# Four single PSUM banks in place of two bank pairs in the gate and up products of a hybrid encoder

## The chip, the cores and the metric

The kernel runs on one core of one Trainium2 chip. The metric is the device time of one execution in microseconds, as the median of several runs. TensorE (PE) does the matrix products; its sequence of weight loads is shown apart as PEld. VectorE (DVE) and ScalarE (ACT) read PSUM, GpSimd (POOL) works in SBUF alone, and SyncE (SP) issues most of the DMAs.

## The reference, cut to what matters

Two encoder layers, 1024 tokens of width 1024 in fp32. Each layer has a mixer stage, a gated MLP and a gated input embedding. The change touches the first two products of the MLP:

```python
D_FF = 2816
for i in range(DEPTH):                      # DEPTH = 2
    ...
    gate = dwconv_centred(h @ ffn_w_gate[i], ffn_conv_w[i], ffn_conv_b[i])
    f = (jax.nn.silu(gate) * (h @ ffn_w_up[i])) @ ffn_w_down[i]
    h = layer_norm(ALPHA * h + f, ln2_g[i], ln2_b[i])
    ...
```

## The kernel before, in words

**Work and tiles.** The kernel is written with pools of tiles; a scheduler then sets the order of the instructions on each engine, from the program's order and from what each one must wait for. Each fp32 operand is split into a high and a low part (`split`, L82: ACT copies the high part, another engine subtracts), and one product of two such operands is three matmuls (`p3`).

**The gate and up products** are in `gate_up` (L1355), once for each layer. The 2816 hidden features are taken in 22 blocks of 128. One block's up weights and gate weights together are a matrix of two block rows; the tokens' transposed activations are cut in two by two blocks. Block by block, they are multiplied by a scheme with seven products instead of eight: `product` (L1380) is 4 times `p3`, that is 12 matmuls of 128x128 by 128x512 into one PSUM bank of 128x512 fp32. Seven operands on the token side are kept for the whole stage: the tiles named `x` in the trace are B11, B21, 22 and t1, and those named `xq` are t2, t3 and t4. The weight side is made anew for each feature (`feature`, L1398): two DMAs bring the raw up and gate weights (`wraw`), sums and differences are taken, and `part` (L1375) splits them into the tiles `w`. For the first three features the two products with B11 and B21 are made ahead (`starts`, L1466), while the other token operands are still being built from transposes (L1473 to L1486).

**PSUM.** There are eight banks. The pool `ps1` gives single banks (tile `ps`, four of them, `one()`), the pool `ps2` pairs of banks (tile `pp`, two of them, `two()`). In `feature` two pairs are taken: `pa` (L1413) takes the product with t2 in its first half and that with t1 in its second, `pb` (L1426) that with t4 and that with 22. The products with t3, B11 and B21 take single banks:

```python
pa = self.two()
u = small()
self.tt(u, product(w2, B["t2"], pa[:, lo]), v1, add)
u4 = small()
self.tt(u4, product(w1, B["t1"], pa[:, hi]), u, add)
```

Each product is read from PSUM by DVE, which adds it to an earlier result (tiles `u`, `v`, `g`); the one with B11 is copied by ACT (`v1`).

**What follows a feature.** `gated` (L1432) takes the convolution and the SiLU of the gate and multiplies by up; `paired` (L1444) stores sums and differences of two features to DRAM (`fp`, from the tiles `u` and `k`) for the down projection. The down projection (`down_paired`, from L1546 on; its matmuls are L1613) starts with operands called `part`, made of `fr` (read back from `fp`) and of the down weights (`wr`, `wraw`); its first product takes both bank pairs.

**Queues.** SP issues its DMAs in the order in which the scheduler put them, weight loads and stores among each other, and a DMA whose data is not ready holds up those behind it.

Of the kernel before, what the change touches and what calls it, by code (L numbers as in the profile page):

```python
# [2 lines left out]

# [7 lines left out]
F32 = mybir.dt.float32  # L11
# [4 lines left out]
PSUM = bass.MemoryType.PSUM  # L16
# [58 lines left out]
class Trunk:  # L75
# [32 lines left out]

    def two(self):
        return self.ps2.tile([128, 1024], F32, name="pp", tag="pp")  # L110

    def load_w(self, src, shape, pool=None, tag="whl", eng=None, bufs=None):
        nc = self.nc
        raw = self.wp.tile(shape, F32, name="wraw", tag="wraw", bufs=2)
        nc.sync.dma_start(raw, src)
        pool = pool or self.wp
        kw = {"bufs": 4} if pool is self.wp else {"bufs": bufs} if bufs else {}
        hi = pool.tile(shape, F32R, name="wh", tag=tag, **kw)
        lo = pool.tile(shape, F32R, name="wl", tag=tag, **kw)
        self.split(hi, lo, raw, eng or nc.gpsimd)  # L120
        return hi, lo
# [107 lines left out]
    def build(self):  # L229
        tc, ctx = self.tc, self.ctx  # L230
        self.ps1 = self.pool(ctx, "ps1", 4, space=PSUM)
        self.ps2 = self.pool(ctx, "ps2", 2, space=PSUM)
        self.dram = self.pool(ctx, "dram", 1, space=DRAM)
        self.sm = self.pool(ctx, "sm", 2)
        self.small_constants()
        self.wp = self.pool(ctx, "wp", 2)
        self.xp = self.pool(ctx, "xp", 8)
        self.khat = [[self.dram.tile([128, 3 if q == 0 else 2, 512], F32, name=f"khat{l}_{q}")
                      for q in range(8)] for l in range(L)]
        x = None  # L240
        for l in range(L):
            with ExitStack() as st:
                mu = self.pool(st, f"mu{l}")
                late = None
                if l == 0:
                    x, late = self.embed()
                else:
                    x, late = nxt
                rows = self.mixers(l, x, mu, late, st)
            hst = ExitStack()  # L250
            mid = self.out_proj(l, hst, *rows)
            nxt = self.rest(l, hst, *mid)
# [1102 lines left out]
    def gate_up(self, l, H, hp, x, fd):  # L1355
# [4 lines left out]
        add, sub = ALU.add, ALU.subtract  # L1360
        fd, fp = fd
        kept = []
        with ExitStack() as st:
# [4 lines left out]
            B = {"11": x[0], "21": x[1]}  # L1368

            def load(n, f):  # L1370
                w = self.wp.tile([128, 1024], F32, name="wraw", tag="wraw", bufs=2)
                nc.sync.dma_start(w.rearrange("p (k m) -> p k m", k=8), t[n][l, f])
                return w[:, 0:512], w[:, 512:1024]
# [3 lines left out]
                self.split(w[:, 0], w[:, 1], src, eng or nc.gpsimd)  # L1377
                return w

            def product(w, b, ps=None):  # L1380
                ps = self.one() if ps is None else ps
                wh, wl = [w[:, i].rearrange("p (k m) -> p k m", k=4) for i in range(2)]
                self.mm(ps, [z for k in range(4) for z in self.p3(wh[:, k], wl[:, k], b[0][:, k], b[1][:, k])])
                return ps

            def first(w1, w2, eng=None):

                v1, c11 = small(), fu.tile([128, 512], F32, name="u", tag="u", bufs=6)
                self.act(v1, product(part(w1, self.wp, "whl", eng), B["11"]))

                def second():
                    self.tt(c11, product(a12, B["21"]), v1, add)
                    return c11

                a12 = part(w2, self.wp, "whl", eng)
                return v1, second

            def feature(f, last, start=None):  # L1398
                a11, a12 = load("ffn_w_up", f)
                a21, a22 = load("ffn_w_gate", f)  # L1400
                v1, c11 = start or first(a11, a12)
                s1 = fu.tile([128, 512], F32, name="s", tag="s", bufs=1)
                self.tt(s1, a21, a22, add)
                w1 = part(s1, hp, "H")
                self.tt(a21, a11, a21, sub)
                self.tt(a11, s1, a11, sub, nc.gpsimd)
                w2 = part(a11, hp, "H", nc.vector)
                w3 = part(a21, hp, "H", nc.vector)
                w22 = part(a22, hp, "H")
                self.tt(a12, a12, a11, sub, nc.gpsimd)  # L1410
                w4 = part(a12, hp, "H")
                lo, hi = slice(0, 512), slice(512, 1024)
                pa = self.two()  # L1413
                u = small()
                self.tt(u, product(w2, B["t2"], pa[:, lo]), v1, add)
                u4 = small()
                self.tt(u4, product(w1, B["t1"], pa[:, hi]), u, add)
                if last:
                    gated(*last)
                g = big()  # L1420
                p7 = product(w3, B["t3"])
                self.tt(g[:, 512:1024], p7, u4, add)
                self.tt(u, p7, u, add)
                if start is None:
                    c11 = c11()
                pb = self.two()  # L1426
                self.tt(g[:, 0:512], product(w22, B["t4"], pb[:, lo]), u, add)
                c12 = fu.tile([128, 512], F32, name="u", tag="u", bufs=6)
                self.tt(c12, product(w4, B["22"], pb[:, hi]), u4, add)
                return f, g, c11, c12  # L1430

            def gated(f, g, *cc):  # L1432
                tg = big()
                self.conv3(tg, g, pp[:, C_FFC + 4 * f:C_FFC + 4 * f + 4])
                self.act(tg, tg, AF.Silu)
                for hf, c in enumerate(cc):
                    cs = slice(hf * 512, (hf + 1) * 512)
                    self.tt(c, c, tg[:, cs], ALU.mult, nc.gpsimd if hf else nc.vector)
                    if f >= PAIRED:
                        nc.sync.dma_start(fd[f][:, cs], c)  # L1440
                if f < PAIRED:
                    paired(f, *cc)
# [21 lines left out]
                    put(3, s4)  # L1464

            starts = []  # L1466
            for f in range(3):
                v1, c11 = first(*load("ffn_w_up", f), nc.vector)
                starts.append((v1, c11()))
# [3 lines left out]
            for j in range(4):  # L1473
                h0, h1 = H[j], H[j + 4]
                a, b = slice(0, 512), slice(512, 1024)
# [9 lines left out]
                self.blocks([(d[:, b], p2[:, a], B["t3"]), (d[:, a], p2[:, b], B["t2"])], j)  # L1485
                self.blocks([(h0[:, b], self.one(), B["t4"])], j)  # L1486
            last = None
            for f in range(NF):
                last = feature(f, last, starts[f] if f < 3 else None)
            gated(*last)  # L1490

    def down(self, l, fd, hmid, H, end, ed):
        nc, t, pp = self.nc, self.t, self.pp[l]
# [341 lines left out]
```

## Time and profile before

| | us |
|---|---|
| median of 3 runs | 3204.69 |
| these runs | 3196.22 to 3207.54 |
| the profiled execution, its own time | 3194.46 |
| its span | 3192.7 |
| PE busy in the span | 2946.4 (92%) |
| DVE busy | 2440.4 (76%) |
| POOL busy | 1771.2 (55%) |
| ACT busy | 1291.6 (40%) |
| gate and up, layer 0: from the first product with a token operand made of a transpose to the end of the last | 813.8 to 1245.0 |
| gate and up, layer 1: the same | 2390.5 to 2822.0 |

An engine that waits is idle in these numbers, so the share of busy time says which engine is nearest to being the bound, but not which waits matter. The ends of matmuls are modelled in the trace, so the pace of PE is best read from the starts of matmuls that follow each other. The granted clock of TensorE is either full (2.4 GHz, shown as 1.00) or half (1.2 GHz), and a stretch shows the mean.

### The profile page before, as it was taken

To read this page: it belongs to the slowest core of one execution; us is meant where nothing else is said; L and a number is where in the kernel's file an instruction comes from. 1 tells how busy PE (TensorE), PEld (TensorE's weight loads), DVE (VectorE), ACT (ScalarE), POOL (GpSimd) and SP (SyncE) were. 2 spreads that over 40 slices of the span, in tenths; PEclk is the share of its full clock that TensorE was granted. 3 is DMA by queue.
4 is the path that set the end of the run, shared out by engine and by line. 5 is a ranking of instruction groups with operands and counts; after the bars stand their busy time and mean duration, and the time that the engine had idled before them with its cause. 6 is when DMAs were issued, how large, how long until landed. Compare 5 with 4: busy or idle time off the path is not lost.

```text
span 3192.7 us, 40546 instructions
## 1 busy us (share of the span) xinstructions
PE 2946.4 (92%) x14316; PEld 2420.9 (76%) x14316; DVE 2440.4 (76%) x3711; ACT 1291.6 (40%) x2278; POOL 1771.2 (55%) x1371
## 2 busy tenths in 40 slices
PE   6999988999899999999989998889989999999996
PEld 4887866877678777787867877768767787777785
DVE  7678786878766777889777786868786677768986
ACT  4332365743333334443342333667333333344341
POOL 5455533527555666887435463335185556679845
PEclk9999998999999999999999998999999999999998
DMA  5466523022233326523335664130322333274332
GB/s 181 152 202 213 180 85 137 16 84 86 76 99 106 102 96 225 189 93 124 114 107 159 219 215 158 53 122 17 107 73 83 99 111 99 101 257 146 106 132 89
DMA packets 153427, 400.44 MB, mean 125 GB/s; under 512 B 16578, under 2 KB 43462, under 8 KB 152968
## 3 DMA queue, kind: packets, MB, share of 16 engines
q1 hardware_dynamic: 138968, 347.18, 32.5%
q0 software_dynamic: 14256, 50.67, 5.2%
q8 instruction: 114, 1.87, 0.2%
q14 instruction: 89, 0.73, 0.1%
HBM read 294.50 MB, written 103.28 MB: 125 GB/s over the span
## 4 chain that ended last, share of the span: by engine, by line
PE 48%; DVE 22%; POOL 9%; DMA 8%; issue 8%; ACT 5%; SPq 0%; DVEq 0%; POOLq 0%; ACTq 0%
PE ps L99 17%; PE pp L99 15%; PE ps L1613 7%; DMA wraw<-in_ffn_w_gate_dram 4%; POOL H L87 2%; DVE g L90 2%; DVE u L87 2%; PE ps L942 2%; DVE w L87 2%; POOL w L87 2%; DVE H L90 2%; PE ps L1054 1%; DVE v L87 1%; ACT w L84 1%; POOL wraw L87 1%
## 5 line engine op out<-in xcount | busy, mean ns | idle before, releaser
L99 PE MATMUL pp<-x,wh 128*128 128x512 f32 x1344 | 430.0, 398 | 1.8 <-ACT wh L84 1.8
L1613 PE MATMUL ps<-part 128*128 128x512 f32 x1440 | 341.4, 393 | 14.7 <-DVE H L87 6.1
L87 POOL TENSOR_TENSOR w<-wraw,w 128x512 fp32r<-128x512 f32 x164 | 232.7, 1431 | 206.0 <-ACT w L84 205.8
L1613 PEld LDWEIGHTS ps<-part 128*128 128x128 f32 x1440 | 270.8, 189 | 78.4 <-DVE H L87 9.8
L99 PEld LDWEIGHTS pp<-x,wh 128*128 128x128 f32 x1344 | 256.1, 193 | 54.2 <-ACT wh L84 2.0
L99 PE MATMUL ps<-x,w 128*128 128x512 f32 x1056 | 261.6, 395 | 10.8 <-ACT v L84 10.8
L99 PE MATMUL pp<-x,w 128*128 128x512 f32 x1056 | 258.3, 394 | 14.1 <-DVE v L87 9.7
L99 PE MATMUL pp<-x,wl 128*128 128x512 f32 x672 | 266.8, 397 | 3.8 <-POOL wl L87 3.8
L99 PE MATMUL pp<-xq,w 128*128 128x512 f32 x1056 | 264.4, 392 | 5.8 <-DVE x L87 4.5
L84 ACT ACTIVATE w<-wraw 128x512 fp32r<-128x512 f32 x264 | 152.8, 622 | 267.6 <-DMA wraw<-in_ffn_w_up_dram 169.9
L87 POOL TENSOR_TENSOR wl<-wraw,wh 128x1024 fp32r<-128x1024 f32 (+2 forms) x61 | 153.6, 2520 | 173.6 <-ACT wh L84 119.8
L99 PEld LDWEIGHTS pp<-x,w 128*128 128x128 f32 x1056 | 196.9, 188 | 63.7 <-DVE v L87 13.8
L87 POOL TENSOR_TENSOR part<-fr,part 128x512 fp32r<-128x512 f32 x140 | 220.5, 1602 | 43.7 <-ACT part L84 43.4
L99 PEld LDWEIGHTS ps<-x,w 128*128 128x128 f32 x1056 | 199.0, 190 | 59.9 <-ACT v L84 18.0
L99 PEld LDWEIGHTS pp<-xq,w 128*128 128x128 f32 x1056 | 198.0, 188 | 51.2 <-ACT w L84 5.1
L99 PE MATMUL ps<-wo,yn 128*128 128x512 f32 x768 | 188.0, 401 | 5.5 <-DVE H L90 3.1
L87 DVE TENSOR_TENSOR part<-wr,part 128x512 fp32r<-128x512 f32 x124 | 155.5, 1278 | 39.0 <-ACT part L84 38.7
L1039 POOL TENSOR_TENSOR P<-P,smr 128x1024 f32<-128x1024 f32 x64 | 121.2, 1895 | 110.1 <-DVE smr L1038 101.2
L99 PEld LDWEIGHTS ps<-wo,yn 128*128 128x128 f32 x768 | 145.4, 193 | 39.6 <-DVE H L90 5.4
L99 PE MATMUL ps<-wh,x 128*128 128x512 f32 x512 | 158.7, 390 | 0.0
L99 PEld LDWEIGHTS pp<-x,wl 128*128 128x128 f32 x672 | 129.1, 192 | 30.6 <-POOL wl L87 4.7
L90 DVE SCALAR_TENSOR_TENSOR g<-g,pp 128x1023 f32<-128x1023 f32 x88 | 128.4, 1460 | 27.0 <-ACT g L84 25.6
(385 smaller groups left out, 7264.5 us busy)
## 6 DMA issues: line engine op xcount, KB each, us to landing
fr<-fp SPq DMA_DIRECT2D x70, 512.0 KB, 3.7
c_fwd<-in_c_fwd_dram POOLq DMA_DIRECT2D x64, 512.0 KB, 5.4
wraw<-in_ffn_w_up_dram SPq DMA_DIRECT2D x50, 512.0 KB, 3.5
fp<-u SPq DMA_DIRECT2D x100, 256.0 KB, 2.4
wraw<-in_ffn_w_gate_dram SPq DMA_DIRECT2D x44, 512.0 KB, 3.8
wraw<-in_w_in_dram SPq DMA_DIRECT2D x42, 512.0 KB, 3.7
wr<-in_ffn_w_down_dram SPq DMA_DIRECT2D x36, 512.0 KB, 4.8
c_inv<-in_c_inv_dram POOLq DMA_DIRECT2D x32, 512.0 KB, 4.8
```

Source lines behind the costliest of these rows:

```text
L84: self.nc.scalar.activation(out, in_, func, **kw)
L87: (eng or self.nc.vector).tensor_tensor(out, a, b, op=op)
L90: return self.nc.vector.scalar_tensor_tensor(out, a, s, b, op0=op0, op1=op1)
L99: ins = self.nc.tensor.matmul(out, a, b, start=i == 0, stop=i == n - 1)
L942: ins = self.nc.tensor.matmul(out[0:64] if j else out, v[:, 0, :] if j else v.rearrange("p i d -> p (i d)"), terms[i][1 + j], start=k == 0 ...
L1039: nc.gpsimd.tensor_tensor(P, P, sm.to_broadcast([128, T]), op=ALU.mult)
L1054: nc.tensor.transpose(pt[:, j * 128:(j + 1) * 128], P[:, c0:c0 + 128], self.ident)
L1613: nc.tensor.matmul(ps, u, v, start=k == 0 and (p != 1 or ch == 0), stop=k == 5 and (p != 1 or ch == last))
```

## The change

From `feature(0)` on, the pool of two bank pairs is closed and a pool of four single banks takes its place (tile `pt`). `product` takes its bank by turns from this pool and from the four `ps` banks; `turn` is constant 0 before that point, so that the products made ahead still take `ps`. After the last `gated` the pairs come back. What is computed is the same; the scheduler orders the changed program anew.

```diff
+    def swap2(self, name, bufs):
+
+        self.st2.close()
+        self.ps2 = self.st2.enter_context(self.tc.tile_pool(name=name, bufs=bufs, space=PSUM, reuse_waits="tile"))
...
         self.ps1 = self.pool(ctx, "ps1", 4, space=PSUM)
-        self.ps2 = self.pool(ctx, "ps2", 2, space=PSUM)
+        self.st2 = ctx.enter_context(ExitStack())
+        self.ps2 = self.pool(self.st2, "ps2", 2, space=PSUM)
...
-            def product(w, b, ps=None):
-                ps = self.one() if ps is None else ps
+            def product(w, b):
+                if next(turn):
+                    ps = self.ps2.tile([128, 512], F32, name="pt", tag="pt")
+                else:
+                    ps = self.one()
...
-                lo, hi = slice(0, 512), slice(512, 1024)
-                pa = self.two()
                 u = small()
-                self.tt(u, product(w2, B["t2"], pa[:, lo]), v1, add)
+                self.tt(u, product(w2, B["t2"]), v1, add)
                 u4 = small()
-                self.tt(u4, product(w1, B["t1"], pa[:, hi]), u, add)
+                self.tt(u4, product(w1, B["t1"]), u, add)
...
-                pb = self.two()
-                self.tt(g[:, 0:512], product(w22, B["t4"], pb[:, lo]), u, add)
+                self.tt(g[:, 0:512], product(w22, B["t4"]), u, add)
                 c12 = fu.tile([128, 512], F32, name="u", tag="u", bufs=6)
-                self.tt(c12, product(w4, B["22"], pb[:, hi]), u4, add)
+                self.tt(c12, product(w4, B["22"]), u4, add)
...
+            turn = itertools.repeat(0)
...
             last = None
+            turn = itertools.cycle((1, 0))
+            self.swap2(f"ps3_{l}", 4)
             for f in range(NF):
                 last = feature(f, last, starts[f] if f < 3 else None)
             gated(*last)
+            self.swap2(f"ps2_{l}", 2)
```

Three places show how the order moves. In all of them the number behind `w_` names one product's weights, and `x12` means twelve matmuls in a row.

**A feature in the steady part, on PE** (layer 0, feature 5). Before, weights 8416 belong to B21, 8421 to t1, 8426 to t2, 8429 to t3 and 8432 to t4 of this feature; 8543 and 8573 are B11 and t3 of feature 6, and 8287 is the last product (with 22) of feature 4. The order before:

```order
L99 MATMUL ps<-x,w_8416 128x512 x12
L99 MATMUL ps<-x,w_8543 128x512 x7
L99 MATMUL pp<-xq,w_8426 128x512 x10
L99 MATMUL pp<-x,w_8287 128x512 x12
L99 MATMUL pp<-xq,w_8426 128x512 x2
L99 MATMUL ps<-x,w_8543 128x512 x5
L99 MATMUL ps<-xq,w_8573 128x512 x12
L99 MATMUL pp<-xq,w_8432 128x512 x9
L99 MATMUL pp<-x,w_8421 128x512 x12
L99 MATMUL pp<-xq,w_8432 128x512 x3
```

The order now, with the seven products of the same feature (B11, t2, t1, t3, B21, t4, 22):

```order
L100 MATMUL ps<-x,w_8413 128x512 x12
L100 MATMUL pt<-xq,w_8440 128x512 x12
L100 MATMUL ps<-x,w_8435 128x512 x12
L100 MATMUL pt<-xq,w_8443 128x512 x12
L100 MATMUL ps<-x,w_8430 128x512 x12
L100 MATMUL pt<-xq,w_8446 128x512 x12
L100 MATMUL ps<-x,w_8450 128x512 x12
```

The two products of a pair, which stood apart with the work of the neighbouring features between them, now stand in the program's order, one feature after the other.

**The same part, on SP**: the loads of feature 6 (up, then gate) and the stores near them (`u` and `k`; k_8332 before and k_8345 now are the `k` of feature 3). Before:

```order
L1372 DMA wraw_8537<-in_ffn_w_up_dram 128x1024
L1446 DMA fp0_7499<-u_8230 128x512
L1446 DMA fp0_7499<-u_8086 128x512
L1372 DMA wraw_8539<-in_ffn_w_gate_dram 128x1024
L1446 DMA fp0_7499<-u_7585 128x512
L1446 DMA fp0_7499<-k_8332 128x512
```

Now:

```order
L1379 DMA wraw_8553<-in_ffn_w_up_dram 128x1024
L1453 DMA fp0_7499<-u_7585 128x512
L1453 DMA fp0_7499<-k_8345 128x512
L1379 DMA wraw_8555<-in_ffn_w_gate_dram 128x1024
L1453 DMA fp0_7499<-u_8261 128x512
L1453 DMA fp0_7499<-k_8491 128x512
```

The gate load has moved behind the last stores of feature 3.

**The start of the stage, on PE** (layer 0, behind the last transposes). Before, 7793, 7796 and 7799 are t2, t3 and t4 of feature 0, and 7893 is t3 of feature 1:

```order
L1281 MATMUL pp<-ident,g 128x128 x8
L99 MATMUL ps<-xq,w_7796 128x512
L99 MATMUL pp<-xq,w_7793 128x512
L99 MATMUL ps<-xq,w_7796 128x512 x11
L99 MATMUL pp<-xq,w_7793 128x512 x11
L99 MATMUL pp<-xq,w_7799 128x512 x12
L99 MATMUL ps<-xq,w_7893 128x512 x11
```

Now, 7792, 7797, 7800 and 7803 are t1, t2, t3 and t4 of feature 0:

```order
L1288 MATMUL pp<-ident,g 128x128 x8
L100 MATMUL ps<-x,w_7792 128x512
L100 MATMUL ps<-xq,w_7803 128x512 x12
L100 MATMUL ps<-x,w_7792 128x512 x11
L100 MATMUL pt<-xq,w_7797 128x512 x12
L100 MATMUL pt<-xq,w_7800 128x512 x12
```

PE now begins with the products with t1 and t4, in `ps`, and comes to t2 and t3 after them. At the end of the stage, where the last gate and up product used to stand between the first two groups of twelve L1613 matmuls, it now stands ahead of all of them.

## Rows read from the trace of the kernel before

**Rows 1.** Page, part 1: busy us, share of the span and instructions of each engine.

```profile
PE 2946.4 (92%) x14316; PEld 2420.9 (76%) x14316; DVE 2440.4 (76%) x3711; ACT 1291.6 (40%) x2278; POOL 1771.2 (55%) x1371
```

**Rows 2.** Windows, both stages: us, then PE, PEld, DVE, ACT, POOL busy, clock, DMA.

```profile
813.80:1245.00 431.20, 416.19 (x1788) 335.25 (x1788) 308.70 (x345) 144.42 (x213) 241.63 (x170) 1.00 0.34 112
2390.50:2822.00 431.50, 416.71 (x1788) 335.31 (x1788) 309.03 (x345) 144.45 (x214) 241.84 (x170) 1.00 0.34 112
```

**Rows 3.** Timeline, PE, steady stretch: start us, us, what, [idle before and releaser].

```profile
1011.04 2.91 PE L99 MATMUL pp<-xq,w 128*128 128x512 f32 x12
...
1022.03 2.91 PE L99 MATMUL pp<-xq,w 128*128 128x512 f32 x12
```

**Rows 4.** Groups by line, PE, layer 0's stage: busy us, mean ns, idle before and releasers.

```profile
L99 PE MATMUL pp<-xq,w 128*128 128x512 f32 x528 | 132.1, 392 | 3.0 <-DVE x L87 2.3 <-DVE v L87 0.5
L99 PE MATMUL pp<-x,w 128*128 128x512 f32 x528 | 129.0, 393 | 7.1 <-DVE v L87 4.8 <-DVE g L87 2.3
L99 PE MATMUL ps<-x,w 128*128 128x512 f32 x456 | 112.6, 392 | 2.4 <-ACT v L84 2.4
L99 PE MATMUL ps<-xq,w 128*128 128x512 f32 x264 | 67.5, 400 | 3.3 <-DVE xq L87 1.4 <-DVE w L87 1.1 <-ACT xq L84 0.8
```

**Rows 5.** Groups by line, PE, layer 1's stage.

```profile
L99 PE MATMUL pp<-xq,w 128*128 128x512 f32 x528 | 132.3, 392 | 2.8 <-DVE x L87 2.1 <-DVE v L87 0.6
L99 PE MATMUL pp<-x,w 128*128 128x512 f32 x528 | 129.3, 394 | 7.0 <-DVE v L87 4.9 <-DVE g L87 2.0
L99 PE MATMUL ps<-x,w 128*128 128x512 f32 x456 | 112.5, 392 | 2.2 <-ACT v L84 2.2
L99 PE MATMUL ps<-xq,w 128*128 128x512 f32 x264 | 67.6, 400 | 3.3 <-DVE xq L87 1.4 <-DVE w L87 1.1 <-ACT xq L84 0.8
```

**Rows 6.** Timeline, DVE and PE, two waits in layer 0's stage.

```profile
1143.50 0.68 DVE L87 TENSOR_TENSOR g<-pp,v 128x512 f32<-128x512 f32 x1
...
1144.24 3.03 PE L99 MATMUL pp<-x,w 128*128 128x512 f32 x12 [1.34 <-DVE g L87]
...
1150.89 0.68 DVE L87 TENSOR_TENSOR v<-pp,v 128x512 f32<-128x512 f32 x1
...
1151.62 3.04 PE L99 MATMUL pp<-x,w 128*128 128x512 f32 x12 [1.60 <-DVE v L87]
```

**Rows 7.** Timeline, ACT, DVE and PE, start of layer 0's stage.

```profile
812.20 1.08 ACT L84 ACTIVATE x<-pp 128x512 fp32r<-128x512 f32 x2 [0.66 <-PE pp L1281]
...
815.23 1.28 DVE L87 TENSOR_TENSOR x<-pp,x 128x512 fp32r<-128x512 f32 x2
...
816.66 0.47 PE L99 MATMUL pp<-xq,w 128*128 128x512 f32 x1 [2.33 <-DVE x L87]
817.81 1.27 DVE L87 TENSOR_TENSOR xq<-pp,xq 128x512 fp32r<-128x512 f32 x2
...
818.54 4.31 PE L99 MATMUL ps<-xq,w 128*128 128x512 f32 x11 [1.41 <-DVE xq L87]
```

**Rows 8.** Timeline, PE, first waits of the down projection, layers 0 and 1.

```profile
1246.07 3.37 PE L1613 MATMUL ps<-part 128*128 128x512 f32 x12 [1.08 <-ACT part L84]
...
1258.11 10.06 PE L1613 MATMUL ps<-part 128*128 128x512 f32 x36 [3.23 <-DVE H L90]
...
2823.89 4.81 PE L1613 MATMUL ps<-part 128*128 128x512 f32 x12 [2.03 <-ACT part L84]
...
2835.92 14.45 PE L1613 MATMUL ps<-part 128*128 128x512 f32 x61 [1.61 <-DVE H L90]
```

**Rows 9.** Timeline, SP and DVE, from loads to weights and from a product to its store.

```profile
1002.58 0.38 SPq L1372 DMA_DIRECT2D wraw<-in_ffn_w_gate_dram  x1
...
1009.64 0.69 DVE L87 TENSOR_TENSOR g<-pp,v 128x512 f32<-128x512 f32 x1
...
1010.98 1.82 DVE L87 TENSOR_TENSOR w<-wraw,w 128x512 fp32r<-128x512 f32 x2 [0.64 <-ACT w L84]
...
1025.71 0.32 SPq L1446 DMA_DIRECT2D fp<-k  x1
```

More of the change, by code (lines that the diff above doesn't have):

```diff
@@ L1 @@
+import itertools
 import math
```

## The prediction

> **What bounds the kernel now.** The page's first part says that PE is busy for 92% of the span and DVE for 76% [rows 1], so PE comes first. The change touches two stretches only, so I read those next, as two windows: the gate and up stage takes 431.2 us in layer 0 and 431.5 us in layer 1, with 1788 matmuls in each: 148 products of 12, and 12 that belong to the down projection [rows 2]. How fast PE could go there is read from a stretch without a wait: five groups of twelve follow each other, and from the start of the first, 1011.04, to the start of the fifth, 1022.03, 48 matmuls take 10.99 us, or 0.2290 us each [rows 3]. At that pace 1788 matmuls take 409.4 us. So 21.8 us of layer 0's stage and 22.1 us of layer 1's are not work but waiting and its after-effects: 43.9 us in all. The stage is bound by PE, and that is the most that a better order inside it can give back.
>
> What the waits are is in the groups by line. In layer 0 the products into bank pairs (`pp`) wait 7.6 us for DVE's reads of `v` and `g`, and 2.3 us for DVE's `x`; those into `ps` wait 2.4 us for ACT's copy `v`, 1.4 us for `xq` and 1.1 us for weights [rows 4]. Layer 1 repeats it: 7.5, 2.1, 2.2, 1.4 and 1.1 us [rows 5]. The two lines on `v` and `g` show what waits for what: DVE reads the first half of a pair from 1143.50 to 1144.19, and PE starts the product into the second half at 1144.24; DVE reads until 1151.57, PE starts at 1151.62 [rows 6]. The second product of a pair waits until the first one has been read, although it goes to another bank. Pair and order belong together: the order before puts about three other products between the two of a pair to cover that read, and where the cover is too short, PE stands still.
>
> **The change, part by part.**
>
> *The pair waits go.* Each product gets a tile of its own, so a read of one product no longer holds the next. What could hold PE is a bank that has not been read when its turn comes again: eight banks by turns come round after eight products, 8 x 12 x 0.2290 = 22.0 us, of which 2.7 us are the writing, so DVE may be 19 us late. DVE is busy for 308.7 of 431.2 us there [rows 2], so 19.2 us per feature leave it 5.5 us free and it has no reason to fall that far behind. So I take the waits for `v` and `g` as gone, 7.6 + 7.5 = 15.1 us, and with them the waits in `ps` for ACT's copy, 2.4 + 2.2 = 4.6 us, since its bank too now has seven others before it is wanted again. Bounds: 0, if the reads come later by as much as the banks allow, and 19.7 us. I take 19.7: in [rows 6] PE goes on within 0.1 us of a read that it could have had 19 us of room for.
>
> The Trainium skill, "TensorE: Matmul & The Clock Gate", section "HAM oscillation — how this bites in real kernels", speaks against a gain of this kind: in the kernel measured there, double-buffering PSUM gave nothing more. By that rule this term would be 0 and the sum below 12.6 us. The trace does not agree so far: here PE waits for reads of PSUM in rows of its own.
>
> *Each wait's after-effect goes.* The twelve matmuls after such a wait take 3.03 or 3.04 us [rows 6] where twelve in a row take 2.91 [rows 3], 0.12 us more. There are 13 such waits in layer 0's timeline and 11 in layer 1's (two stand in rows 6): 24 x 0.12 = 2.9 us.
>
> *The start.* Before, PE began with t3 and t2, whose low parts come last: it waited 2.33 us until DVE's `x` had been read out of a pair, ran one matmul, and waited 1.41 us for `xq`, until 818.54 [rows 7]; 2.1 and 1.4 us in layer 1 [rows 5]. Now it begins with t1, whose high part is ready at 813.28, and t4, whose transposes come earlier; those 12 matmuls last until about 816.3, t1's low part is there at 816.51, its other 11 matmuls last until 819.0, and t2's and t3's low parts are there at 819.08 [rows 7]. About 0.3 us of waiting is left in each layer: 7.2 - 0.6 = 6.6 us gained. It is 0 if the transposes finish later. The new pool can give no bank before the pairs have been read at the start, and that is the same 819.08, so I cost the swap at nothing. The cover is those 24 matmuls; without it the swap would cost the 3.7 us per layer that the start waits today.
>
> *The end.* The down projection's second operand made PE wait 1.08 and 2.03 us [rows 8]; 12 of its matmuls had already been used up ahead of the last gate and up product. Now all 24 of the first operand stand behind it, 5.5 us of work in place of 2.7, which covers both waits: 3.1 us. The waits for DVE's `H` that follow, 3.23 and 1.61 us [rows 8], I leave as they are. Bounds: 0, and 7.9 us if all four go.
>
> *Weights.* The wait for weights, 1.1 us a layer, I leave. The order on SP makes a gate load stand behind the last stores of the feature three before it. I cost this at nothing, because the load has room. From a feature's sum `g` to its last store, 1009.64 to 1025.71, are 16.1 us, and from a gate load to split weights, 1002.58 to 1012.80, 10.2 us [rows 9]: 26.3 us in a row. From the end of that earlier feature to the first product with these weights PE has two features and one product, 15 x 2.75 = 41 us. The cover is 15 us; a load that is later than that stops PE, and then DVE's sums, which stand behind the same feature's `s` in its queue, are late next.
>
> The sum: 19.7 + 2.9 + 6.6 + 3.1 = 32.3 us, say 32. Against the profiled execution's 3194.46 us that gives 3162. The median of the runs is 10 us above that execution, and I go from the median: 3204.7 - 32 = **3172 us**. What a measurement of this kernel can tell from no change is about 0.5%, 16 us.
>
> **The rivals.**
>
> *The stops move, they do not go.* PE's wait for DVE's read comes back elsewhere, at the banks or at weights, because the same sums stand in DVE's queue behind loads (`s`, `w`). For it: DVE is busy for 72% of the stage [rows 2]. Against it: the 19 us of room. Then only start and end remain, 9.7 us: 3195 us, no change that can be told.
>
> *Slower: the gate load behind the stores.* Place: SP, in each of the 19 features after the third, both layers. Price: each us by which the split gate weights come too late costs PE 38 us. It decides beyond the 15 us of cover, and makes the kernel slower by over 16 us from 48 / 38 = 1.3 us late on, with the 32 us spent; at 1.5 us late, 3204.7 - 32 + 57 = 3230 us. Against it: the trace has the load with room to spare.
>
> *The clock.* If PE fell to half clock through short stops at every change of bank, each fall would add time. At the stage's start, after the waits there, PE's 11 matmuls from 818.54 took 4.31 us, 0.39 each in place of 0.229 [rows 7]; elsewhere in the windows the clock shows full [rows 2], through all the waits counted above. One fall with a dozen slow matmuls, 2 us, in each of 38 features would be 76 us: about 3249 us. The Trainium skill, "TensorE: Matmul & The Clock Gate", section "A second HAM failure mode: psum-queue depth-cycling", describes this: a kernel that cycles through PSUM banks idles briefly between groups and the clock swings. The trace does not show it for short waits.
>
> *More is gained.* All 43.9 us of the stage and the 7.9 us at the two ends go: 3153 us.
>
> **How the numbers follow.** The forecast has 0.68, the stops that move 0.19, more gained 0.07, the late loads 0.04, the clock 0.02. The forecast and the greater gain are faster by over 16 us, except for a small part of the forecast in which the end and the start give nothing and some waits stay, 0.02: 0.73. The same: 0.19 + 0.02 = 0.21. Slower: 0.06. The range reaches from all that can be gained, 3153, to 3196, just beyond the case in which only start and end are left; outside lie the late loads, the clock and a little of each end.
>
> **What would show it.** Right: each stage takes 412 to 416 us, PE has no line of waits for `v` or `g` there, and the stage's first products run from 813.4 on without a wait above 0.5 us. Groups of twelve start every 2.75 us in the program's order. Wrong, step by step: waits of `pt` or `ps` for DVE or ACT over 3 us in a layer (the banks are not free in time); PE waiting for ACT's or POOL's `w` (the loads); a granted clock below 1.00 within the steady part; a wait longer than 3 us ahead of the first L1613 matmuls (the swap back to pairs, or the operands). If the stages shrink as said and the median does not, the time went into the down projection, whose first operands come from stores and loads of their own.

## The result, and the profile after

The changed kernel takes 3242.66 us (median of 4 runs, 3239.6 to 3248.53) against 3205.6 us for the kernel before (4 runs as well): **1.2% slower**, ratio 1.0124 with a 95% interval of 1.0099 to 1.0148. The forecast was 3172 us, range 3153 to 3196. The profiled execution shown here took 3248.53 us.

The page's first part, after. PE is busy for 22 us longer than in [rows 1], in a span that is 54 us longer:

```profile
PE 2968.5 (91%) x14316; PEld 2432.7 (75%) x14316; DVE 2461.4 (76%) x3711; ACT 1293.6 (40%) x2278; POOL 1828.7 (56%) x1371
```

Two stretches of layer 0's steady part as windows (columns: window, length, busy time and count of matmuls on PE, then the other engines), first after, then before:

```profile
1000.00:1100.00 100.00, 94.36 (x400) 75.19 (x399) 68.13 (x75) 31.00 (x47) 56.84 (x37) 0.98 0.28 94
1100.00:1200.00 100.00, 90.70 (x387) 71.58 (x387) 68.03 (x75) 33.66 (x50) 59.79 (x38) 1.00 0.24 81
```

```profile
1000.00:1100.00 100.00, 99.43 (x433) 80.81 (x433) 73.19 (x85) 34.80 (x52) 58.23 (x43) 1.00 0.35 114
1100.00:1200.00 100.00, 93.83 (x405) 75.18 (x404) 76.45 (x78) 33.75 (x50) 62.78 (x41) 1.00 0.27 91
```

At PE's pace of [rows 3], 100 us hold 437 matmuls. After, 37 and 50 are missing; before, only 4 in the first stretch, but 32 in the second. So the kernel before, too, lost its pace late in the stage, and not to its start or end.

What PE waits for between 834 and 1258, by the view of waits (total us, times, longest us); this answers to [rows 4]:

```profile
PE ps L100 <- ACT w L85: 12.9, 8, 2.4
PE ps L100 <- DVE u L88: 8.1, 7, 1.2
PE pt L100 <- DVE v L88: 2.9, 7, 0.4
```

The waits of the pairs are gone, as forecast, and 23.9 us of others stand in their place. The start did as forecast, counted from the last transposes (in this execution the whole stage begins some 5 us later); the timeline's first products have no wait beside them, where [rows 7] had 2.33 and 1.41:

```profile
819.01 2.91 PE L100 MATMUL ps<-xq,w 128*128 128x512 f32 x12
821.76 2.68 PE L100 MATMUL ps<-x,w 128*128 128x512 f32 x11
824.28 5.66 PE L100 MATMUL pt<-xq,w 128*128 128x512 f32 x24
```

The end did the opposite. In place of 1.08 and 3.23 us [rows 8] the down projection's first products wait for 2.92, 3.03 and 4.49 us:

```profile
1260.40 7.32 PE L1624 MATMUL pp<-part 128*128 128x512 f32 x24 [2.92 <-DVE v L88]
1270.74 5.71 PE L1624 MATMUL ps<-part 128*128 128x512 f32 x16 [3.03 <-ACT part L85]
1280.94 3.78 PE L1624 MATMUL ps<-part 128*128 128x512 f32 x8 [4.49 <-DVE part L88]
```

**What sets the pace.** The chain of waits, followed back from the end of the stretch, has no PE in it. Its summary for layer 1, 2440 to 2800, and two features of it (start, length, what; "issue" is time in which the engine's wait is not resolved further):

```profile
by line: issue 25.1%; POOL wraw L88 14.4%; DMA wraw<-in_ffn_w_up_dram 10.3%; DMA wraw<-in_ffn_w_gate_dram 8.7%; POOL w L88 8.1%; POOL u L88 7.1%; DVE k L88 5.0%; DVE u L88 4.0%; ACT w L85 2.7%; DVE v L88 1.5%; DVE s L88 1.4%; SPq L1453 1.3%
...
2509.34 4.19 DMA wraw<-in_ffn_w_gate_dram
...
2513.55 0.70 DVE s L88
...
2517.63 2.17 POOL wraw L88
2519.80 3.54 issue
...
2523.37 1.81 POOL u L88
...
2525.21 1.79 DVE k L88
...
2527.44 3.71 DMA wraw<-in_ffn_w_up_dram
...
2531.89 3.57 POOL w L88 x3
...
2537.91 2.16 POOL wraw L88
2540.07 4.14 issue
...
2544.25 1.81 POOL u L88
...
2551.23 4.64 DMA wraw<-in_ffn_w_gate_dram
```

From one gate load to the second after it are 2551.23 - 2509.34 = 41.9 us, 20.9 per feature. Over the whole stage it is more: layer 0's sixth gate load goes out at 882.84, its twenty-second at 1223.90, and (1223.90 - 882.84) / 16 = 21.3 us; PE needs 84 x 0.2290 = 19.24.

What "issue" hides is in the timelines. One feature on DVE, ACT, POOL and SP, in this order:

```profile
1081.71 0.69 DVE L88 TENSOR_TENSOR s<-wraw 128x512 f32<-128x512 f32 x1 [2.75 <-DMA wraw<-in_ffn_w_gate_dram]
...
1085.16 1.63 DVE L91 SCALAR_TENSOR_TENSOR g<-g,pp 128x1023 f32<-128x1023 f32 x1 [1.38 <-ACT g L85]
...
1087.31 1.78 DVE L88 TENSOR_TENSOR w<-wraw,w 128x512 fp32r<-128x512 f32 x2
1089.02 1.27 DVE L91 SCALAR_TENSOR_TENSOR g<-g,pp 128x1023 f32<-128x1023 f32 x1
...
1090.38 1.06 ACT L85 ACTIVATE g<-g 128x1024 f32<-128x1024 f32 x1 [3.00 <-DVE g L91]
1091.35 1.14 ACT L85 ACTIVATE w<-wraw 128x512 fp32r<-128x512 f32 x2
...
1085.78 2.16 POOL L88 TENSOR_TENSOR wraw<-wraw 128x512 f32<-128x512 f32 x1
1091.52 1.80 POOL L88 TENSOR_TENSOR u<-u,g 128x512 f32<-128x512 f32 x1 [3.58 <-ACT g L85]
1093.29 3.02 POOL L88 TENSOR_TENSOR w<-wraw,w 128x512 fp32r<-128x512 f32 x2
...
1095.17 0.32 SPq L1453 DMA_DIRECT2D fp<-k  x1
...
1096.33 0.33 SPq L1379 DMA_DIRECT2D wraw<-in_ffn_w_gate_dram  x1
```

This is a loop, called **the load loop** below. Gate weights land, and DVE sums them (`s`, 1081.71). Behind `s` in DVE's queue stands the gating of the feature two before: two steps of its convolution (`g`, 128x1023), with the splits `w2` and `w3` of the new feature between them. The SiLU follows on ACT (1090.38), the multiply on POOL (`u<-u,g`, 1091.52). Only behind these stand the new feature's last two splits, `w22` and `w4` (1091.35 on ACT, 1093.29 on POOL). POOL was through with what they read at 1087.94, so POOL's part of them starts about 5 us later than it could. When they are done, at 1096.31, the raw buffers are free, and the next gate load goes out at 1096.33. There are two buffers, for one feature, so no turn can start before the last has ended.

A second way back to the load hangs on the same multiply: DVE's `k` (1093.36) needs its result, the store of `k` goes out on SP at 1095.17, and the loads behind it on SP wait for it. In the chain above it is this way (DVE `k`, SPq L1453) that ends last; in the feature shown here the two ways end about 1 us apart.

DVE falls behind PE until the bank that PE wants next has not been read; then PE waits for DVE's reads. At the end of the stage PE has to wait until DVE has caught up.

### The profile page after: what moved, and what is told of

It is laid out like the page before. It is cut to its first block, busy times and chain, and to the rows that moved or that the text cites. A ratio compares the mean times of both kernels' runs of the same rounds, so it can differ in the third digit from the quotient of the medians.

```text
span 3246.7 us, 40664 instructions
## 1 busy us (share of the span) xinstructions
PE 2968.5 (91%) x14316; PEld 2432.7 (75%) x14316; DVE 2461.4 (76%) x3711; ACT 1293.6 (40%) x2278; POOL 1828.7 (56%) x1371
## 5 line engine op out<-in xcount | busy, mean ns | idle before, releaser
L100 PE MATMUL ps<-x,w 128*128 128x512 f32 x1176 | 287.8, 395 | 20.4 <-DVE u L88 13.8
L100 PEld LDWEIGHTS ps<-x,w 128*128 128x128 f32 x1176 | 221.8, 190 | 74.4 <-issue 18.6
L100 PE MATMUL pt<-x,w 128*128 128x512 f32 x936 | 227.3, 392 | 1.3 <-DVE u L88 1.2
L100 PE MATMUL ps<-xq,w 128*128 128x512 f32 x744 | 189.5, 405 | 28.7 <-ACT w L85 28.7
L100 PE MATMUL pt<-xq,w 128*128 128x512 f32 x840 | 205.1, 393 | 5.3 <-DVE v L88 5.3
L100 PEld LDWEIGHTS pt<-x,w 128*128 128x128 f32 x936 | 175.4, 188 | 42.5 <-ACT v L85 4.9
L100 PEld LDWEIGHTS ps<-xq,w 128*128 128x128 f32 x744 | 142.4, 194 | 67.6 <-ACT w L85 35.0
L100 PEld LDWEIGHTS pt<-xq,w 128*128 128x128 f32 x840 | 156.6, 188 | 44.7 <-DVE v L88 11.4
```

Of the source, the lines that this page charges most:

```text
L100: ins = self.nc.tensor.matmul(out, a, b, start=i == 0, stop=i == n - 1)
```

## The experiments

Most change the order of instructions alone, by edges that set the order of issue on one engine and wait for nothing: `behind(late, early)`. `made` holds the ACT and the POOL (or DVE) instruction of the last `part`, in e1 the gate load. e4 and e12 also leave out work, e7 and e8 also deal the banks out otherwise, and e6 and e10 start from the kernel before, where the scheduler orders PE's products differently too. In the others PE's order is the changed kernel's, word for word. The diffs show the edges and not the lines that collect the instructions. Three theories stood against each other: LOOP, the load loop; BANKS, DVE's order of reading the banks by itself; STORES, the gate load behind the stores on SP, the prediction's slower rival. Spacing is that of layer 0's gate loads from the sixth to the twenty-second, as above.

| run | median, us | ratio to before (95%) | spacing, us |
|---|---|---|---|
| the kernel before | 3205.6 | 1 | 19.67 |
| the changed kernel | 3242.66 | 1.0124 (1.0099 to 1.0148) | 21.32 |
| e1 loads first | 3230.53 | 1.0102 (1.0084 to 1.0121) | 21.30 |
| e2 splits first | 3156.13 | 0.9862 (0.9842 to 0.9881) | 18.56 |
| e3 early read | 3232.12 | 1.0100 (1.0081 to 1.0119) | 21.01 |
| e4 less PE | 3210.93 | 1.0037 (1.0024 to 1.0051) | 20.69 |
| e5 convolution first | 3197.43 | 0.9993 (0.9979 to 1.0008) | 19.77 |
| e6 pairs, splits first | 3169.54 | 0.9900 (0.9884 to 0.9917) | 19.01 |
| e7 no turns | 3250.78 | 1.0164 (1.0139 to 1.0188) | 21.19 |
| e8 no turns, splits first | 3172.22 | 0.9909 (0.9894 to 0.9925) | 18.83 |
| e9 convolution and loads first | 3168.58 | 0.9905 (0.9883 to 0.9927) | 19.23 |
| e10 pairs, slow order | 3264.38 | 1.0199 (1.0181 to 1.0218) | 21.48 |
| e11 splits and convolution first | 3155.17 | 0.9862 (0.9841 to 0.9882) | 18.62 |
| e12 splits first, less PE | 3107.74 | 0.9711 (0.9681 to 0.9740) | 17.60 |

The kernel before was run again beside each group of runs (medians 3198.49 to 3201.62), so runs of different groups are compared by their ratios; 0.0010 is 3.2 us. The mean spacing of e2 and those like it is below 19.24 because the loads first run ahead of PE and only then fall in with it.

**e1, the loads ahead of the stores.** In `feature`, behind the gate load (`sto` holds the stores of each feature):

```diff
+                for late in sto.get(f - 3, ()):
+                    self.behind(late, made[0])
```

> The changed kernel with one thing forced: SP issues the gate load of a feature ahead of the stores of the feature three before it. Three theories on why the change is slower (3242.66 against 3205.6 us). LOOP: the stage is paced by a loop without PE (load, sums and splits, SiLU and multiply of the gate, the last two splits behind that multiply, raw buffer free, next load), 21.1 us per feature in the changed kernel's trace where PE needs 19.24; in every second turn the gate load stands 2.2 us behind stores (1075.41 to 1077.60), so about 1.1 us per feature goes: stage about 18 us shorter in each layer, 3205 us (3195 to 3225). BANKS: DVE reads a bank so late that PE has to wait for it, and the order of DVE's reads alone decides: no change, 3243 (3235 to 3250). STORES: the loads behind the stores are the whole cause (the slower rival of the prediction): all of the loss goes and the gain comes, 3180 (3165 to 3195).

Nearly nothing came: STORES falls as the whole cause, and LOOP's size for it was wrong. By the ratios it is 7 us faster than the changed kernel, which the two intervals don't tell from nothing. The chain for layer 1 shows why. The gate load now goes out as soon as POOL's last splits end, but it takes 5.76 and 5.45 us to land where it took 4.19 and 4.64, and the turn is as long as before, now by way of the last splits: 2540.21 - 2518.89 = 21.3 us.

```profile
2518.89 2.99 POOL w L88 x2
...
2521.90 5.76 DMA wraw<-in_ffn_w_gate_dram
...
2532.07 2.16 POOL wraw L88
2534.23 4.14 issue
...
2538.41 1.80 POOL u L88
2540.21 2.99 POOL w L88 x2
...
2543.22 5.45 DMA wraw<-in_ffn_w_gate_dram
```

**e2, the last splits ahead of the SiLU and the multiply.** Behind `w4`:

```diff
+                if f >= 2:
+                    self.behind(sil[f - 2], made[0])
+                if f >= 2:
+                    self.behind(mul[f - 2], made[1])
```

> The changed kernel with two things forced: ACT and POOL make the last two splits of a feature's weights (w22, w4) ahead of the SiLU and the multiply of the feature two before it, and as a result the scheduler also puts the loads ahead of the stores, as in the run with the loads first. PE's order is unchanged. LOOP: the raw buffers come free some 6 us earlier (POOL is ready at 1066.4, the splits end at 1075.4 in the trace), the loop falls below PE's 19.24 us per feature, PE becomes the bound, the gate and up stage takes 415 to 422 us and the time is 3165 us (3150 to 3180). BANKS: the reads keep their order, 3240 (3230 to 3250). STORES: the same as with the loads first alone, within 5 us.

LOOP's number was met, 9 us to the better. SP's order is that of e1 but for a few rows, so what e2 gains over e1, 74 us, does not come from the stores. It comes with the order on ACT and POOL, and with what the scheduler moved on DVE: some reads of PSUM now stand ahead of DVE's multiply, which waits for the SiLU. Among each other DVE's reads keep the changed kernel's order to the row, and so does PE, so BANKS, which expected no change from that, falls here; e5 leaves the reads behind the multiply and is the cleaner test. The chain for layer 1, 2440 to 2740, is now PE alone, and in layer 0 the window from 1100 to 1200 holds 440 matmuls:

```profile
by line: PE pt L103 50.2%; PE ps L103 49.8%
```

```profile
1100.00:1200.00 100.00, 100.00 (x440) 82.28 (x439) 74.35 (x84) 36.68 (x52) 63.13 (x42) 1.00 0.34 107
```

This kernel beats both: 1.4% below the one before. PE's waits for banks are gone, with the same banks, turns and reads as in the changed kernel.

**e3, one bank read earlier.** On DVE `s` is put behind the sum that reads the product with B21 of the feature two before:

```diff
+                for early in sums.get(f - 2, ()):
+                    self.behind(s_ins, early)
```

> The changed kernel with one thing forced: DVE reads the product with B21 (the sum into u) ahead of the sum s of the feature two later, which waits for a gate load. Nothing moves on PE, ACT, POOL and SP. BANKS: PE's wait for that bank (about 1.2 to 1.5 us in every second feature, 28.7 us in all, put down to ACT's w by the profile) goes, and the time falls to about 3212 us (3200 to 3225). LOOP: the period stays at 21.1 us per feature, since PE isn't in the loop; the wait comes back at another bank; 3243 (3233 to 3250). STORES: no change.

It is 8 us faster than the changed kernel by the ratios, and the spacing is 21.0: nearer to LOOP, which expected nothing, than to BANKS, which expected some 30. PE's waits in layer 0, over the same stretch as above:

```profile
PE pt L104 <- DVE v L88: 10.8, 8, 1.5
PE ps L104 <- DVE u L88: 3.4, 7, 0.5
PE pt L104 <- DVE g L88: 2.7, 5, 0.9
```

The 12.9 us that the profile had put down to ACT's `w` are gone, though ACT's order is the same: it was this read of a bank by DVE that ended them. At other banks the waits for DVE's `v` grew from 2.9 to 10.8 us, and the rows shown add up to 16.9 us in place of 23.9. About half of the wait came back elsewhere and the spacing hardly fell, so this wait is not the cause.

**e4 and e12, less work for PE.** The product with t3 leaves out the four matmuls of the weights' low part, in e4 in the changed kernel, in e12 in that of e2:

```diff
-... for z in self.p3(wh[:, k], wl[:, k], b[0][:, k], b[1][:, k])])
+... for z in self.p3(wh[:, k], wl[:, k], b[0][:, k], b[1][:, k])[:2 if cut else 3]])
```

> The changed kernel with less work for PE: the product with t3 leaves out its four matmuls of the weights' low part (8 matmuls in place of 12, so the output lacks that part), 0.92 us less per feature, 40 us in all. The scheduler orders the rest nearly as before. LOOP: the steady part stays at about 21 us per feature; only where PE is the bound, in the first five or six features of each layer, is something gained: 3230 us (3220 to 3240). BANKS (a chain through PE: product, late read, next product): most of the 40 us goes, 3205 (3195 to 3215). STORES: as LOOP.

> The run with the splits first (3156 us) with less work for PE: the product with t3 leaves out the four matmuls of the weights' low part, 0.92 us less per feature, 40 us in all. In the changed kernel the same cut gave 3211 us, some 28 us less, with gate loads still 20.5 to 20.7 us apart where PE then needed 18.3. LOOP: here PE is the bound, so nearly all of it comes: gate loads about 18.3 to 18.6 us apart, 3120 us (3114 to 3130). Rival, ANOTHER BOUND NEAR BY (DVE, busy for three quarters of the stage, or the loop at 18.6): less than half comes, 3137 us or more.

e12 gained 48 us, more than the 40 taken away: there PE is the bound. The rest lies outside the stage: the stretch between the two layers' stages, in which nothing is changed, is 9.5 us shorter in its profile than in e2's. e4 gained 28 us by the ratios, where LOOP expected 12, and its 3210.93 us lie in the range of BANKS; 12 us of the gain are again in that stretch. Its spacing stayed at 20.7, far above the 18.3 us that PE then needs. The scheduler had moved other things as well: in every second feature one of the splits `w2` and `w3` went behind the convolution's second step, and the chain of e4 shows that turn with a shorter wait of POOL ahead of `u`, 2.94 us in place of 4.14:

```profile
2535.18 2.94 issue
...
2554.78 3.54 issue
```

That fits the loop, but e4 alone does not tell it from BANKS. e5 does.

**e5, the convolution ahead of two splits.** On DVE alone; ACT, POOL and SP keep their order too. Behind `w2` and again behind `w3`:

```diff
+                if f >= 2:
+                    self.behind(made[1], conv[f - 2])
```

> The changed kernel with one thing forced, on DVE alone (PE, ACT, POOL and SP keep their order word for word): the second step of the gate's convolution (g, 128x1023) comes ahead of the two splits w2 and w3 of the feature two later, behind which it stood. LOOP (load, s, convolution, SiLU, multiply, last splits, raw buffer free, load; no PE in it): two splits and the wait for ACT's high parts leave the loop, about 2.8 and 2.3 us in the two features of a pair by the trace (the second step starts at 65.3 in place of 68.1, at 86.7 in place of 89.0), 21.3 to about 18.7 us per feature, below PE's 19.24: gate loads 19.2 us apart, 3165 us (3150 to 3185). BANKS (only the order of the reads of PSUM matters, and these keep theirs): no change against the changed kernel, 3238 (3228 to 3246).

The reads of PSUM keep their order among each other to the row, and 42 us came by the ratios. Not the whole, though: the spacing is 19.8, not 18.7. What was left showed in its loads, 18.5 and 21 us apart by turns, the long turn with the stores of `u` and `k` ahead of the gate load. So **e9** adds the edit of e1:

> The changed kernel with both single edits: on DVE the second step of the convolution ahead of the splits w2 and w3 of the feature two later, and on SP the gate load ahead of the stores. Alone the first gave 3197 us (gate loads 18.5 and 21.1 us apart by turns, 19.8 and 20.1 in the mean), the second nothing that counts. LOOP: the turn of 21.1 us is the one in which the load stands behind stores of u and k; without them it falls to about 19 (the two loads then start together and land a little later), so PE becomes the bound: gate loads 19.2 us apart, 3170 us (3158 to 3182). Rival, NO SECOND STEP (loads first gives nothing, as alone): 3197 (3190 to 3203).

3168.58 us, 19.23 us apart: PE's pace. (The 14 us that e9 stays above e2 are not in the steady part: at the start of layer 0's down projection PE waits 3.65 and 3.46 us, in e2 3.94.) The stores cost nothing while another part of the loop is as long, and 28 us once it is not. **e11** put the convolution first in e2's order:

> The run with the splits first (3156 us, gate loads 19.2 us apart) with the convolution's second step ahead of the splits w2 and w3 on DVE as well. LOOP: PE is the bound already, so a shorter loop gives nothing more in the steady part; 3155 us (3148 to 3162). Rival, LATE READS: waits at the end of the stage (4.0 us for DVE's part in layer 1) shrink because DVE is less behind: 3148 (3142 to 3152).

Nothing: the ratio is that of e2. A loop that is shorter than PE's work is worth nothing more.

**e6 and e10, the same orders with the bank pairs.** e6 is the edit of e2 in the kernel before. e10 forces the slow order on it: the convolution's second step behind `w3`, the last two splits behind SiLU and multiply (the scheduler also moves PE's products there):

```diff
+                if 2 <= f < NF:
+                    self.behind(conv[f - 2], made[1])
...
+                if f >= 2:
+                    self.behind(made[0], sil[f - 2])
+                    self.behind(made[1], mul[f - 2])
```

> The kernel before, with its bank pairs, and the same two things forced as in the run with the splits first (last two splits of a feature ahead of the SiLU and the multiply of the feature two before it; the loads then come ahead of the stores by the scheduler's choice). It tells what single banks are worth when the load loop is not the bound. LOOP: the loads that came 20.5 us apart late in the stage come at PE's pace; the waits at the pairs stay, as the prediction counted them (19.7 us and 2.9 us after-effects): 3182 us (3172 to 3192), some 26 us above the singles with the same order. Rival, ORDER ALONE: the waits at the pairs were only the loop's doing and go with it: 3160 us (3150 to 3168), the single banks are worth nothing.

> The kernel before, with its bank pairs, forced into the order that the changed kernel has around the gating: on DVE the second step of the convolution behind the splits w2 and w3 of the feature two later, on ACT and POOL the last two splits behind the SiLU and the multiply in every feature. LOOP (the order of these makes the loss, not the banks): gate loads about 21 us apart from the sixth feature on, as in the changed kernel, and the time rises to 3235 us (3225 to 3255). BANKS (single banks and their turns make the loss): no more than 10 us above the kernel before, 3200 to 3210.

e10 is 66 us slower than the kernel before: the order makes the loss, with the pairs in place, and a bigger one than the changed kernel's and than LOOP expected. PE's moved products may have a share in it, which was not tried. e6 gains 30 us with the pairs in place. Its waits for `v` and `g` in layer 0, 834 to 1240, where the kernel before has 5.4 and 2.3 us over that stretch:

```profile
PE pp L102 <- DVE v L87: 0.6, 1, 0.6
PE pp L102 <- DVE g L87: 0.4, 1, 0.4
```

Between e6 and e2, with the splits first in both, lie 0.0038 in the ratio, 12 us: what single banks by turns, with the order on PE that comes with them, are worth here. They lie at the start: of layer 0's matmuls e6 does 25 fewer than e2 between 820 and 840, 18 fewer from there to 870, and 5 fewer in the 330 us behind that. The windows 820 to 840 of e6 and of e2:

```profile
820.00:840.00 20.00, 16.46 (x62) 12.61 (x61) 8.29 (x11) 5.13 (x9) 6.46 (x5) 0.83 0.20 65
```

```profile
820.00:840.00 20.00, 20.00 (x87) 16.18 (x88) 14.20 (x18) 5.50 (x9) 9.75 (x7) 1.00 0.18 59
```

**e7 and e8, no turns.** The products with t2, t1, t4 and 22 take the new banks, the others `ps`; e8 has the edit of e2 as well:

```diff
-                if next(turn):
+                if pair and next(turn):
...
-            turn = itertools.cycle((1, 0))
+            turn = itertools.repeat(1)
```

> The changed kernel without the turns: the products with t2, t1, t4 and 22 take the four new single banks, those with B11, t3 and B21 the four ps banks, as the pairs were shared out before. POOL and SP keep the changed kernel's order (4 lines of POOL differ). LOOP: the banks don't matter, gate loads 21.3 us apart, 3238 us (3228 to 3248). BANKS: the ps banks come round after 4 of 3 products per feature, 1.3 features in place of 1.14, the new ones after exactly one feature, so waits for reads change: 3220 or 3255, beyond 10 us from the changed kernel.

> As the run without turns, with the last two splits forced ahead of the SiLU and the multiply. LOOP: PE-bound as with turns, 3156 us (3146 to 3166), no difference from the turns. Rival, TURNS MATTER: at PE's pace a bank has one feature of room (19.2 us) in place of 22.0, and DVE's late reads cost waits: 3170 to 3190.

e7 keeps the loop and its spacing, 21.2. The turns are worth 13 us in e7 against the changed kernel, where the intervals overlap, and 15 us in e8 against e2, where they don't. So LOOP's expectation for both was too plain, and e8's time is the one that its rival gave. The rival's mechanism, waits for banks, does not show, though: between 834 and 1220 PE has no wait in e8, and its loads are 19.2 us apart as in e2. It is the start and the end again. With the turns t1 and t4 stand in `ps`, and PE begins with them; without them only t3 does, PE begins with t3, and its low part comes late. The first products in e2, then in e8:

```profile
820.29 2.92 PE L103 MATMUL ps<-xq,w 128*128 128x512 f32 x12
```

```profile
823.98 4.84 PE L103 MATMUL ps<-xq,w 128*128 128x512 f32 x11 [3.60 <-DVE xq L88]
```

e8 has done 62 matmuls between 820 and 840, as with the pairs, and its ratio, 0.9909, can't be told from e6's, 0.9900. So four single banks without the turns are worth nothing that shows; what the change has to give is mostly which products PE can begin with.

## Why the prediction was wrong, step by step

Two steps failed: the loads were costed at nothing because "the load has room", and DVE was said to have "no reason to fall that far behind". The runs showed a load loop of 21.3 us a feature in their place, 2.1 us more than PE needs, some 33 us over the 16 features measured in layer 0.

- **The pair waits (-19.7) and their after-effects (-2.9).** They went, and it did not matter. The step failed at "it has no reason to fall that far behind". Busy for 308.7 of 431.2 us, DVE was read as having 5.5 us to spare per feature; but it stands still behind `s`, which waits for a load, and what it has to spare is lost there. The two rows that were to prove the case [rows 6] have the answer one row earlier, in the kernel before:

```profile
1142.89 0.69 DVE L87 TENSOR_TENSOR s<-wraw 128x512 f32<-128x512 f32 x1 [3.01 <-DMA wraw<-in_ffn_w_gate_dram]
```

  DVE's read at 1143.50 was late because `s` had waited 3.01 us for a gate load, and the read at 1150.89 stands behind the same `s`. In e6, where the loop is shorter, the pairs cost 1.0 us in layer 0 in place of 7.7. The term was mostly a symptom of the loop, and about 2 us of it were to be had.
- **The start (-6.6).** Right, and somewhat more: 87 - 62 = 25 matmuls in the windows above are 25 x 0.2290 = 5.7 us in one layer, since e6's PE also shows a granted clock of 0.83 there after its waits.
- **The end (-3.1).** Wrong in sign in the changed kernel, 10.4 us of waits in place of 4.3 in layer 0, because the stage ends with DVE far behind. In e2 the products of the down projection start 0.2 us after the last of the stage (1225.52 and 1225.74), but at 1238.91 PE still waits 3.94 us for DVE's `part`, so the sum of these waits is hardly below that of the kernel before.
- **The weights (0).** This step missed the cause. It set a way of 26.3 us against a cover of 41 us and found 15 us of room. But a cover hides a delay, not a rate: with raw buffers for one feature, each turn starts when the last one ends, and the question was whether a turn, 21.3 us, is longer than PE's 19.24. The signs for that were there: loads and splits in [rows 9], and the 405 matmuls of the second window of the kernel before.
- **The pool swap (0).** Right at the start, where no wait shows at it. At the end, where the pairs come back, the 2.92 us in the changed kernel end with DVE's read `v` of a single bank; in e2 this wait is gone.
- **The rivals.** "The gate load behind the stores" had the right queue, but only one of the two ways through the loop: e1 took the stores away and nearly nothing came. "The stops move" is what PE's waits did, but as a sign of the loop. The clock hardly swung: 0.98 and 1.00 in the windows, where one group of twelve was slowed, 4.57 us at 1018.71, behind a wait of 2.35 us. Most of "more is gained" was there to be had (e2: 3156.13 us), by an order that the change did not bring.
- **The rule.** The Trainium skill, "TensorE: Matmul & The Clock Gate", section "HAM oscillation — how this bites in real kernels", says of the kernel measured there that double-buffering PSUM gave no further gain. By that rule the sum was at most 12.6 us. The 12 us between e6 and e2 side with it against the 32 us. That the two numbers meet is luck: 12.6 was start, end and after-effects, and the 12 us lie at the start.

What a scheduler makes of a change is part of the change. With the pairs gone it put the convolution's second step behind both splits, and POOL's multiply ahead of both last splits, in every feature from the fourth on. In layer 0 of the kernel before the first holds for the first 13 features and the second for four late ones, where that kernel lost its pace, but never both for one feature. Why its plan preferred that was not looked into. Nor is all of the profiled difference of 54 us placed: the stretch from the end of layer 0's down projection to layer 1's first gate load, in which nothing is changed, differs by 5.8 us between the two profiles, and over the profiles of all these runs by up to 13; the stretch up to layer 0's first gate load differs by 4.9 us.

## What to carry to other kernels

Follow a wait one step further than the engine it names: that engine may itself have stood behind an instruction that waited for a load. For each buffer that is used again, add up one turn of its loop (load, use, all that stands ahead of the last use in its queues, free, next load) and set it against the pace of the bounding engine; a busy share of 76% says nothing about it. After a change in pools, compare the orders on every engine, and fix the few that close such a loop by hand: here two edges for each feature turned 1.2% slower into 1.4% faster.

## What was not expected of the hardware

In e1, where stores follow a gate load on SP within half a us, it took 5.76 and 5.45 us to land, with the stores ahead of it 4.19 and 4.64. That the stores slow it was not tried, and e2 speaks against it: there a store follows 0.55 us behind, and the loads at 2619.01 and 2657.35 took 4.17 and 4.12 us, with the up load 2.25 us ahead of them and not 1.72 as in e1.

DVE and POOL instructions on SBUF can take longer when both work: in the changed kernel POOL's subtraction into `wraw` took 2.16 us at 1085.78 and that of the same size before it 1.30, and DVE's `k` took 1.78 us at 1093.36, beside POOL's splits, and 0.67 at 1076.48 with POOL idle. So work that is moved off the path could still make the path longer; no run here tried that alone.
